# Hybrid-decoder step on one core: dilated attention's loads joined (both heads, both halves), v kept a second time by residue, and two SBUF pools exchanged

## The chip, the cores and the metric

The kernel runs on one core of a Trainium2 chip, as one launch. The metric is the device time of that launch in microseconds. Before the change it is 3003.89 us, the median of three runs (3002.21 to 3005.41).

## The reference, cut to what matters

One decoder layer is computed for 2048 prompt tokens and for 32 new tokens of eight running requests, all in float32. `h + concat(HGRN2, DilatedAttention) @ w_o`, then a gated convolutional FFN, then a per-layer embedding gate. The change lies in the prompt's dilated attention:

```
DILATIONS = ((128, 1), (512, 4), (2048, 16))
for window, dil in DILATIONS:
    # positions of one residue class mod dil form a sub-sequence;
    # a query reads the last window/dil + 1 entries of its own
    s = where(valid, q*scale @ k.T, -1e30); m = s.max(-1); p = exp(s - m)
    parts.append((m, p.sum(-1), p @ v))
w = exp(ms - ms.max(0))
out = (w[..., None] * accs).sum(0) / (w * ls).sum(0)[..., None]
```

There are 8 heads of 64 numbers. The kernel works on four pairs of heads p, and on four chunks c of 512 tokens.

## The kernel before, in words

The program has three stretches, told apart in the profile by their lines.

**Input projection (up to about 826 us).** `in_phase` runs twice, on two blocks of tokens, and multiplies the normalised input with seven groups of weights. `token_group` handles q, k, v and i by tiles of 128 tokens: 24 matmuls (L345 to L347), a scaled copy into `ev` (L358), for q and k a rotation and four transposes into `oT`, and then stores into DRAM scratch. L374 stores a tile of q or k into `qT_d` or `kT_d`, laid out [128 rows of a head pair, 4 pairs, 2048 tokens], so that a tile makes runs of 512 bytes. L383 and L384 store a tile of v to its output and to `v_d` [2048, 512].

**Attention (about 826 to 1195 us).** `attn_phase` goes through the four pairs. For each pair and chunk:

- `stage` (L684 to L693) brings q and k in, two tiles [128 partitions, 2 heads, 512]. Both halves of the partitions get the same data, so that one matmul can multiply two precision parts of q. It takes four DMAs, one for each half of each tile, 256 KB each. Pool `a_d` holds four such tiles. `stack` (L695) splits them into `qS`, `kH` and `kL` on ACT and POOL.
- `values_chunk` (L726) brings v in twice: for di = 0 as [128, 4 residues, 128] in one DMA (L731), for di = 1 with the rows of a residue side by side, in four DMAs of 32 partitions (L734).
- 16 `Block`s of 128 queries each pass through `scores` (L803, matmuls L811 and L812, the masked minimum L816 on DVE, which reads `mask`, and the exponential L817 on ACT), `turned` (transposes L824) and `weighted` (L836).
- `merge` (L740 to L775) joins the two softmaxes of a chunk. Their statistics go to DRAM and come back turned (L889, L742); small steps give 16 rows of coefficients, which go to `coef_d` (L763) and come back spread over the partitions in `cf` [128, 2, 512]: two DMAs, one for each head, each reading 4 KB for 64 partitions (L767). POOL multiplies (L772), DVE or POOL adds (L774), and the result is stored to `mix_d` (L775).

Beside it a second generator, `others`, does the last HGRN2 unit and the attention of the 32 new tokens, which reads 32 tiles of 1 MB each (`skt`, L940 and L976).

**Trunk (from about 1201 us).** `trunk` does w_o, FFN and embedding gate. Its first weights are read into pool `tr`, seven buffers `raw` of 2 KB per partition (L1004), and split into `w` (L181, L182); its first activations come from `mix_d` (L1098) and are split by L1080 and L1081.

**What sets the order.** In the attention stretch PE's order is written out by the program. The order on the other engines, and on SyncE (SP), which issues nearly all DMAs, comes from a planner that runs over the whole program. An SP instruction that waits holds up all that stand behind it.

**SBUF.** Pools are put on a stack, each above the one opened before, and a new tile waits for the tiles whose place it takes. Per partition, `early` has 8448 bytes: small constants, the rotary table, at offset 2304 the `mask` of 3072 bytes, then the new tokens' q, k and v. `rows` above it has 8448 bytes: `ssq` and `rb` of the input projection, used again for the very first stage. When attention ends both are closed and the trunk's pools take their place: `ffn_c` 1952 bytes with padding, then `raw` buffer 0 at offset 1952, buffer 1 at 4000, and so on. Buffers 0 and 1 thus lie on the mask.

Of the kernel before, what the change touches and what calls it, by code (L numbers as in the profile page):

```python
# [11 lines left out]
F32 = mybir.dt.float32  # L12
# [10 lines left out]
SEQ = 2048  # L23
# [24 lines left out]
def hymba_step_kernel(ctx: ExitStack, tc: tile.TileContext, I: dict, O: dict):  # L48
    nc = tc.nc
    V, A, G, PE, SP = nc.vector, nc.scalar, nc.gpsimd, nc.tensor, nc.sync  # L50

    const = ctx.enter_context(tc.tile_pool(name="const", bufs=1))
    dram = ctx.enter_context(tc.tile_pool(name="scratch", bufs=1, space=DRAM))

    early_st = ExitStack()
    early = early_st.enter_context(tc.tile_pool(name="early", bufs=1, reuse_waits="tile"))

# [21 lines left out]
    v_s = early.tile([NS, 512], F32, name="v_s")  # L79
    va_s = const.tile([NS, 512], F32, name="va_s")  # L80

    qT_d = dram.tile([128, 4, SEQ], F32, name="qT_d")
    kT_d = dram.tile([128, 4, SEQ], F32, name="kT_d")
    v_d = dram.tile([SEQ, 512], F32, name="v_d")
    va_d = dram.tile([SEQ, 512], F32, name="va_d")
    ha_d = [dram.tile([128, 4, NTOK], F32, name=f"ha{i}_d") for i in range(3)]
# [7 lines left out]
    def f32(ap):  # L94
        return ap.bitcast(F32)
# [89 lines left out]
    recent = []  # L185
# [35 lines left out]
    def in_phase(bi, tiles, shared, wp, ev, sm, pmm, pms, plv, po):  # L221
# [102 lines left out]
        def token_group(g, kind, w):  # L324
            late = None

            for j in (0, 1, 8, 2, 3, 4, 5, 6, 7) if bi else range(8):
                tok = t0 + 128 * j
                n = min(128, T - 128 * j)
                js = slice(128 * j, 128 * j + n)  # L330
                ps = acc_tile()
                smp = n < 128
                if smp:

                    terms = [(xs[:, k], f32(w[k][i])) for k in range(NK) for i in range(2)]
                    side = 128 // n
                    for i, (a, b) in enumerate(terms):
                        c = n * (i % side)
                        PE.matmul(ps[c:c + n], lhsT=a, rhs=b, start=i < side, stop=i >= len(terms) - side,
                                  tile_position=(0, c))  # L340
                else:
                    side = 1
                    for k in range(NK):
                        wh, wl = w[k]
                        PE.matmul(ps, lhsT=xh[k][:, js], rhs=wh, start=k == 0, stop=False)  # L345
                        PE.matmul(ps, lhsT=xh[k][:, js], rhs=wl, start=False, stop=False)  # L346
                        PE.matmul(ps, lhsT=xl[k][:, js], rhs=wh, start=False, stop=k == NK - 1)  # L347
                if late:
                    late()
                    late = None  # L350
                sc = rq if kind == "q" else rc
                if smp and kind == "v":
                    o = v_s
                elif smp and kind == "i":
                    o = va_s
                else:
                    o = ev.tile([128, 512], F32, name="ev", bufs=4)
                A.activation(o[:n], ps[:n], AF.Copy, scale=sc[:n, j:j + 1])  # L358
                for i in range(1, side):
                    V.scalar_tensor_tensor(o[:n], ps[n * i:n * i + n], sc[:n, j:j + 1], o[:n], op0=ALU.mult, op1=ALU.add)  # L360
                if kind in "qk":
                    rotate(o, 16 if smp else tok // 128, n)

                    def late(o=o, n=n, smp=smp, tok=tok):
                        pt = pms.tile([128, 512], F32, name="ms")
                        ptv = pt.rearrange("p (a t) -> p a t", t=128)
                        for p in range(4):
                            PE.transpose(ptv[:, p, :n], o[:n, 128 * p:128 * p + 128], ident[:n, :n])
                        if smp:
                            V.tensor_copy(qT_s if kind == "q" else kT_s, ptv[:, :, :n])  # L370
                        else:
                            oT = ev.tile([128, 4, 128], F32, name="oT", bufs=2)
                            V.tensor_copy(oT, ptv)
                            recent[:] = [SP.dma_start((qT_d if kind == "q" else kT_d)[:, :, tok:tok + 128], oT)]  # L374
                if smp:
                    if kind in "kv":
                        for b in range(8):
                            SP.dma_start(O["s" + kind][b, SEQ - 4:SEQ], o[4 * b:4 * b + 4])
                else:
                    if kind == "k":  # L380
                        SP.dma_start(O["pk"][tok:tok + 128], o)
                    if kind == "v":
                        SP.dma_start(O["pv"][tok:tok + 128], o)  # L383
                        recent[:] = [SP.dma_start(v_d[tok:tok + 128], o)]  # L384
                    if kind == "i":
                        SP.dma_start(va_d[tok:tok + 128], o)
                yield
            if late:
                late()
# [292 lines left out]
    def attn_phase(spare, rest):  # L682

        def stage(p, c, tiles=()):  # L684

            out = []
            for i, src in enumerate((qT_d, kT_d)):
                t = tiles[i] if tiles else dp.tile([128, 2, 512], F32, name="stage", bufs=4)
                for half in range(2):
                    SP.dma_start(t[64 * half:64 * half + 64],  # L690
                                 src[:, p, 512 * c:512 * c + 512].rearrange("(h d) t -> d h t", h=2))
                out.append(t)
            return out  # L693

# [20 lines left out]
        q, k = first  # L715
# [10 lines left out]
        def values_chunk(p, di, c):  # L726

            raw = wk.tile([128, 4, 128], F32, name="v", bufs=6)
            cols = v_d[512 * c:512 * c + 512, 128 * p:128 * p + 128]
            if di == 0:  # L730
                SP.dma_start(raw, cols.rearrange("(i r) c -> i r c", r=4))  # L731
            else:
                for r in range(4):
                    SP.dma_start(raw[32 * r:32 * r + 32], cols.rearrange("(n i r) c -> r i n c", i=32, r=4)[r])  # L734
            vals[p, di, c] = raw

        stats_d = [dram.tile([SEQ, 4], F32, name=f"stat{p}_d") for p in range(4)]
# [2 lines left out]
        def merge(p, c, parts, both):  # L740

            SP.dma_start(both[:, 0].rearrange("p n h c -> p n (h c)"),  # L742
                         stats_d[p][512 * c:512 * c + 512].rearrange("(n i) c -> i n c", i=128))
            stats = both.rearrange("p i n h c -> p c h i n")
            spread = lambda x: x.rearrange("p h (o n) -> p h o n", o=1).to_broadcast([128, 2, 2, 4])
            yield
            mn = sm.tile([128, 2, 4], F32, name="mn")
            w = sm.tile([128, 2, 2, 4], F32, name="w")
            wl = sm.tile([128, 2, 2, 4], F32, name="wl")
            V.tensor_reduce(mn, both.rearrange("p i n h c -> p c h n i")[:, 1], axis=mybir.AxisListType.X, op=ALU.min)  # L750
            G.tensor_sub(w, spread(mn), stats[:, 1])
            A.activation(w, w, AF.Exp)
            yield
            G.tensor_mul(wl, w, stats[:, 0])
            G.tensor_add(mn, wl[:, :, 0], wl[:, :, 1])
            V.reciprocal(mn, mn)
            G.tensor_mul(w, w, spread(mn))
            yield
            ptr = pT.tile([128, 4, 128], F32, name="PT")[:16, 0]
            PE.transpose(ptr, w.rearrange("p h d n -> p (h d n)"), ident)  # L760
            wt = sm.tile([16, 128], F32, name="wt")
            A.copy(wt, ptr)
            SP.dma_start(coef_d[p][c], wt)  # L763

            cf = wk.tile([128, 2, 512], F32, name="cf", bufs=2)
            for h in range(2):
                SP.dma_start(cf[64 * h:64 * h + 64].rearrange("p d i -> p (d i)"),  # L767
                             coef_d[p][c][8 * h:8 * h + 8].rearrange("(o r) i -> o (r i)", o=1)
                             .to_broadcast([64, 1024]))
            yield  # L770
            for i in range(2):
                G.tensor_mul(parts[i], parts[i], cf[:, i])  # L772
            yield
            (G if p == 3 else V).tensor_add(parts[1], parts[1], parts[0])  # L774
            SP.dma_start(mix_d[:, 4 + p, 512 * c:512 * c + 512], parts[1])  # L775
# [73 lines left out]
        n = len(units)  # L849
# [717 lines left out]
    def pools(st, **kw):  # L1567
        def pool(name, bufs, **k):
            return st.enter_context(tc.tile_pool(name=name, bufs=bufs, reuse_waits="tile", **kw, **k))
        return pool  # L1570

    rows_st, in_st, hgrn_st, attn_st = [ExitStack() for _ in range(4)]
    rows = pools(rows_st)("rows", 1)
    pool = pools(in_st)
    args = (in_tiles(pool("xp", 1), rows), [], pool("wp", 9), pool("ev", 2), pool("sm", 1),
            pool("pmm", 2, space=PSUM), pool("pms", 2, space=PSUM))
# [80 lines left out]
        first(side, 1000)  # L1657
    step(main, 1000)
    attn_st.close()
    rows_st.close()  # L1660

    early_st.close()
    with ExitStack() as st:
        pool = pools(st)
        cp = pool("ffn_c", 1)
# [153 lines left out]
```

## Time and profile before

| what | value |
|---|---|
| median of three runs | 3003.89 us |
| the profiled execution's own time | 3008.49 us |
| its span, first to last instruction | 3006.7 us |
| mean TensorE clock granted | 0.981 |
| PE busy | 2908.9 us |
| DVE / ACT / POOL busy | 2166.4 / 1319.2 / 676.9 us |
| DMA moved | 664.14 MB |
| SP issues of `stage` loads after 820 us | 60, of 256 KB |
| SP issues of `cf` loads | 32, of 256 KB |
| SP issues of `v` loads | 16 of 256 KB, 64 of 64 KB |

How to read it: the device time is a little longer than the span, because of what lies around the first and the last instruction. PE's busy share says how near the kernel is to being bound by matmuls, but it is a mean over the three stretches. "DMA share" in the tables below is the mean over the core's 16 DMA engines, so a transfer that keeps two of them busy all the time shows as 0.125. Packets are the single pieces that a DMA engine moves; q1 is the queue into which SP issues.

### The profile page before, as it was taken

The numbers are of one execution on the slowest core, as the hardware profiler recorded it, in microseconds if no ns is written. First come the engines' busy times: TensorE is split into PE (matmuls) and PEld (weight loads), VectorE is DVE, ScalarE is ACT, GpSimd is POOL, SyncE is SP. The second block draws the span as 40 slices with busy tenths as digits, with TensorE's granted clock in tenths as the row PEclk, the third lists the DMA queues.
The fourth block names the chain that finished last, engine by engine and source line by source line (L and its number), as shares of the span: only waits on it lengthen the run. The fifth ranks groups of instructions, "written<-read, shape, count | busy, mean of one in ns | idle before, by whom it ended". The sixth has DMA issues, their size and how long they took to land.

```text
span 3006.7 us, 52441 instructions
## 1 busy us (share of the span) xinstructions
PE 2908.9 (97%) x18895; PEld 2711.0 (90%) x18895; DVE 2166.4 (72%) x4717; ACT 1319.2 (44%) x2856; POOL 676.9 (23%) x792
## 2 busy tenths in 40 slices
PE   8999999999989998999999999999999999999998
PEld 8987789887777677999999999999999999999997
DVE  6656768657386567569988889766769777777777
ACT  5333433222176666335444444544444544444453
POOL 1443222212143463102344431000001000000000
PEclk9999999999989999999999999999999999999998
DMA  5898634323349996766666568677779777778773
GB/s 183 297 359 299 202 103 120 99 86 121 122 107 286 276 249 177 260 224 220 224 206 196 191 198 302 227 252 250 246 230 321 240 242 246 257 249 295 269 274 131
DMA packets 343061, 664.14 MB, mean 221 GB/s; under 512 B 62929, under 2 KB 130641, under 8 KB 341009
## 3 DMA queue, kind: packets, MB, share of 16 engines
q1 hardware_dynamic: 305952, 472.68, 48.4%
q0 software_dynamic: 33264, 121.13, 12.6%
q10 hardware_dynamic: 3584, 66.98, 6.1%
q8 instruction: 149, 2.44, 0.3%
q14 instruction: 112, 0.91, 0.1%
HBM read 513.72 MB, written 213.92 MB: 242 GB/s over the span
## 4 chain that ended last, share of the span: by engine, by line
PE 78%; DVE 9%; DMA 7%; issue 2%; ACT 2%; POOL 1%; SPq 1%; DVEq 0%; POOLq 0%; ACTq 0%
PE mm L143 19%; PE mm L144 19%; PE mm L145 19%; PE mm L345 2%; PE mm L346 2%; PE mm L347 2%; PE acc L836 2%; PE PT L824 2%; PE S L811 1%; DVE h L1305 1%; PE S L812 1%; PE lv L482 1%; DMA wraw<-in_w_in_dram 1%; DMA cf<-coef_d 1%; DMA draw<-in_w_down_dram 1%
## 5 line engine op out<-in xcount | busy, mean ns | idle before, releaser
L144 PE MATMUL mm<-w 128*128 128x348 f32 (+3 forms) x3636 | 1167.6, 322 | 1.9 <-DVE w L1081 1.1
L143 PE MATMUL mm<-w 128*128 128x348 f32 (+3 forms) x3508 | 1111.4, 323 | 21.2 <-ACT s L1247 6.7
L145 PE MATMUL mm<-w 128*128 128x348 f32 (+3 forms) x3508 | 1118.9, 322 | 0.7 <-DVE w L182 0.7
L144 PEld LDWEIGHTS mm<-w 128*128 128x128 f32 x3636 | 685.4, 189 | 4.9 <-DVE w L1081 3.0
L143 PEld LDWEIGHTS mm<-w 128*128 128x128 f32 x3508 | 658.2, 189 | 29.7 <-ACT s L1247 9.3
L145 PEld LDWEIGHTS mm<-w 128*128 128x128 f32 x3508 | 660.2, 189 | 1.8 <-DVE w L182 1.0
L182 DVE TENSOR_TENSOR w<-raw,w 128x512 fp32r<-128x512 f32 x586 | 420.8, 723 | 180.8 <-ACT w L181 175.7
L181 ACT CAST w<-raw 128x512 fp32r<-128x512 f32 x586 | 360.9, 621 | 414.5 <-PE mm L145 286.4
L1289 POOL DMA_DIRECT2D w<-wd_d x231 | 123.8, 536 | 900.1 <-PE mm L145 794.1
L1305 DVE TENSOR_TENSOR h<-h,mm 128x348 f32<-128x348 f32 (+1 forms) x504 | 248.7, 510 | 44.7 <-PE mm L145 43.1
L817 ACT ACTIVATE P<-P,st 128x256 f32<-128x256 f32 (+3 forms) x256 | 134.1, 526 | 67.2 <-DVE st L816 62.6
L1247 ACT COPY s<-mm 128x348 f32<-128x348 f32 (+1 forms) x198 | 87.9, 444 | 158.1 <-PE mm L145 158.0
L816 DVE CUSTOM_DVE_ANT_0 P<-S,mask 128x256 f32<-128x256 f32 (+3 forms) x256 | 104.4, 448 | 62.2 <-PE S L812 39.5
L345 PE MATMUL mm<-wh,xh 128*128 128x512 f32 x352 | 141.0, 404 | 0.0
L346 PE MATMUL mm<-wl,xh 128*128 128x512 f32 x352 | 140.5, 400 | 0.0
L347 PE MATMUL mm<-wh,xl 128*128 128x512 f32 x352 | 140.3, 399 | 0.0
L143 PE MATMUL mm<-xh,wh 128*128 128x384 f32 (+2 forms) x384 | 124.5, 328 | 7.0 <-ACT xh L243 5.0
L145 PE MATMUL mm<-xh,wl 128*128 128x384 f32 (+2 forms) x384 | 124.1, 328 | 4.7 <-DVE wl L268 4.6
L144 PE MATMUL mm<-xl,wh 128*128 128x384 f32 (+2 forms) x384 | 124.8, 327 | 1.3 <-DVE xl L244 1.2
L182 DVE TENSOR_TENSOR dw<-draw,dw 128x512 fp32r<-128x512 f32 x77 | 73.0, 954 | 52.7 <-ACT dw L181 52.6
L149 POOL TENSOR_SCALAR wh<-wraw 128x512 fp32r<-128x512 f32 x96 | 77.4, 820 | 131.6 <-PE mm L144 42.4
L268 DVE TENSOR_TENSOR wl<-wraw,wh 128x512 fp32r<-128x512 f32 x104 | 84.5, 833 | 28.6 <-POOL wh L149 23.3
(346 smaller groups left out, 5090.9 us busy)
## 6 DMA issues: line engine op xcount, KB each, us to landing
w<-wd_d POOLq DMA_DIRECT2D x231, 512.0 KB, 5.5
wd_d<-dw SPq DMA_DIRECT2D x77, 512.0 KB
out_sk_dram<-in_cache_k_dram ACTq DMA_DIRECT2D x56, 584.0 KB
out_sv_dram<-in_cache_v_dram ACTq DMA_DIRECT2D x56, 584.0 KB
raw<-in_w_gate_dram SPq DMA_DIRECT2D x110, 256.0 KB
raw<-in_w_up_dram SPq DMA_DIRECT2D x110, 256.0 KB
wraw<-in_w_in_dram SPq DMA_DIRECT2D x104, 256.0 KB
raw<-w_gate_d SPq DMA_DIRECT2D x88, 256.0 KB
```

The source lines that it names most:

```text
L143: PE.matmul(ps, lhsT=wh, rhs=xh, start=first, stop=False, skip_group_check=read)
L144: PE.matmul(ps, lhsT=wh, rhs=xl, start=False, stop=False, skip_group_check=read)
L145: PE.matmul(ps, lhsT=wl, rhs=xh, start=False, stop=last, skip_group_check=read)
L181: A.copy(w[:, 0], raw)
L182: V.tensor_sub(w[:, 1], raw, f32(w[:, 0]))
L345: PE.matmul(ps, lhsT=xh[k][:, js], rhs=wh, start=k == 0, stop=False)
L346: PE.matmul(ps, lhsT=xh[k][:, js], rhs=wl, start=False, stop=False)
L347: PE.matmul(ps, lhsT=xl[k][:, js], rhs=wh, start=False, stop=k == NK - 1)
L816: V.tensor_tensor_reduce(pe, s[:, w * i:w * i + w], bl.mask, 1.0, 3e38, ALU.add, ALU.min, mn)
L817: A.activation(pe, pe, AF.Exp, bias=mn, scale=-1.0, accum_out=st[:, bl.r, hh, 0:1])
L1289: G.dma_start(t, wd_d[p][n - 1])
L1305: V.tensor_add(o, o, acc[m][:, :H])
```

## The change

`qT_d` and `kT_d` are laid out by chunks, so that the two heads' 512 tokens of one row and chunk stand together as 4 KB, and a tile is stored in two DMAs, one for each head. A stage tile is then filled by one DMA of 512 KB instead of two of 256 KB: its source is the 64 rows of 4 KB, repeated by an outermost dimension of size 2 with step 0. v is stored once more, in `v_r`, with the rows of each 128 ordered by residue, so that the di = 1 load is one DMA too. `cf` is filled by one DMA whose source has the head outermost (2), then 64 repeats of one 4 KB row. Pool `rows` is opened before `early`, so it lies below it.

```
-    qT_d = dram.tile([128, 4, SEQ], F32, name="qT_d")
-    kT_d = dram.tile([128, 4, SEQ], F32, name="kT_d")
+    qT_d = dram.tile([64, 4, 4, 2, 512], F32, name="qT_d")
+    kT_d = dram.tile([64, 4, 4, 2, 512], F32, name="kT_d")
+    v_r = dram.tile([SEQ, 512], F32, name="v_r")
...
-    recent[:] = [SP.dma_start((qT_d if kind == "q" else kT_d)[:, :, tok:tok + 128], oT)]
+    for h in range(2):
+        dst = (qT_d if kind == "q" else kT_d)[:, :, tok // 512, h, tok % 512:tok % 512 + 128]
+        recent[:] = [SP.dma_start(dst, oT[64 * h:64 * h + 64])]
...
-    recent[:] = [SP.dma_start(v_d[tok:tok + 128], o)]
+    SP.dma_start(v_d[tok:tok + 128], o)
+    recent[:] = [SP.dma_start(v_r[tok:tok + 128].rearrange("(r i) c -> i r c", r=4), o)]
...
-    for half in range(2):
-        SP.dma_start(t[64 * half:64 * half + 64],
-                     src[:, p, 512 * c:512 * c + 512].rearrange("(h d) t -> d h t", h=2))
+    half = src[:, p, c].rearrange("(o d) h t -> o d (h t)", o=1)
+    SP.dma_start(t.rearrange("d h t -> d (h t)"), half.to_broadcast([2, 64, 1024]))
...
-    for r in range(4):
-        SP.dma_start(raw[32 * r:32 * r + 32], cols.rearrange("(n i r) c -> r i n c", i=32, r=4)[r])
+    cols = (v_d, v_r)[di][512 * c:512 * c + 512, 128 * p:128 * p + 128]
+    SP.dma_start(raw, cols.rearrange(("(i r) c -> i r c", "(r i) c -> i r c")[di], r=4))
...
-    for h in range(2):
-        SP.dma_start(cf[64 * h:64 * h + 64].rearrange("p d i -> p (d i)"),
-                     coef_d[p][c][8 * h:8 * h + 8].rearrange("(o r) i -> o (r i)", o=1)
-                     .to_broadcast([64, 1024]))
+    SP.dma_start(cf.rearrange("p d i -> p (d i)"),
+                 coef_d[p][c].rearrange("(h o r) i -> h o (r i)", h=2, o=1).to_broadcast([2, 64, 1024]))
...
+    rows_st = ExitStack()
+    rows = rows_st.enter_context(tc.tile_pool(name="rows", bufs=1, reuse_waits="tile"))
     early_st = ExitStack()
...
     attn_st.close()
+    early_st.close()
     rows_st.close()
-
-    early_st.close()
```

More of the change, by code (lines that the diff above doesn't have):

```diff
@@ L728, in values_chunk @@
             raw = wk.tile([128, 4, 128], F32, name="v", bufs=6)
[L729 to L732, printed above, removed]
-                for r in range(4):
-                    SP.dma_start(raw[32 * r:32 * r + 32], cols.rearrange("(n i r) c -> r i n c", i=32, r=4)[r])
+            cols = (v_d, v_r)[di][512 * c:512 * c + 512, 128 * p:128 * p + 128]
+            SP.dma_start(raw, cols.rearrange(("(i r) c -> i r c", "(r i) c -> i r c")[di], r=4))
             vals[p, di, c] = raw
@@ L1570, in pools @@
         return pool
-    rows_st, in_st, hgrn_st, attn_st = [ExitStack() for _ in range(4)]
-    rows = pools(rows_st)("rows", 1)
+    in_st, hgrn_st, attn_st = [ExitStack() for _ in range(3)]
     pool = pools(in_st)
```

## The prediction

> **What bounds the kernel now.** I read the page first, for the engines and the time slices.
>
> ```profile
> span 3006.7 us, 52441 instructions
> PE 2908.9 (97%) x18895; PEld 2711.0 (90%) x18895; DVE 2166.4 (72%) x4717; ACT 1319.2 (44%) x2856; POOL 676.9 (23%) x792
> ...
> PE   8999999999989998999999999999999999999998
> ...
> DMA  5898634323349996766666568677779777778773
> ```
>
> PE is busy for 97% of the span. A slice is 75 us; the DMA engines' three nines, the 13th to the 15th slice, and their peak in the 2nd to 4th are the only places where transfers could be the limit. So I cut the attention stretch out and asked for the busy time in windows. The columns are PE, PEld, DVE, ACT, POOL, granted clock, DMA share, GB/s.
>
> ```profile
> 822.00:850.00 28.00, 19.63 (x92) 16.08 (x91) 19.40 (x57) 15.70 (x37) 20.10 (x18) 0.72 0.88 232
> 850.00:900.00 50.00, 46.82 (x438) 40.80 (x436) 40.04 (x130) 37.23 (x110) 14.54 (x17) 0.94 0.20 45
> 900.00:1100.00 200.00, 186.63 (x1616) 136.38 (x1617) 117.95 (x422) 125.31 (x363) 94.44 (x112) 0.93 0.98 276
> 1100.00:1202.00 102.00, 88.55 (x820) 74.66 (x820) 70.70 (x260) 64.76 (x197) 41.87 (x61) 0.94 0.68 186
> 1202.00:1210.00 8.00, 6.87 (x24) 6.20 (x24) 8.00 (x7) 4.22 (x7) 5.22 (x4) 0.52 0.56 184
> ```
>
> From 900 to 1100 us the 16 DMA engines are 98% busy while PE is 93% busy: there both are near their limit, and DMA has no room to spare. Then the transfers of 822 to 1202 us: the queue's total (packets, MB, share of 16 engines' time) and the loads that the change touches.
>
> ```profile
> q1 hardware_dynamic: 74718, 82.48, 78.1%
> ...
> stage<-qT_d SPq DMA_DIRECT2D x30, 256.0 KB
> ```
>
> ```profile
> cf<-coef_d SPq DMA_DIRECT2D x32, 256.0 KB
> stage<-kT_d SPq DMA_DIRECT2D x30, 256.0 KB
> v<-v_d SPq DMA_DIRECT2D x16, 256.0 KB
> v<-v_d SPq DMA_DIRECT2D x64, 64.0 KB
> ```
>
> 78.1% of 380 us is 297 us of work for each engine, and the 60 stage and 32 cf loads are 92 x 0.262 = 24.1 of the 82.5 MB. Last, what PE itself waited for in that stretch, the first and the fourth row of its list:
>
> ```profile
> PE mm L143 <- ACT w L1080: 6.5, 1, 6.5
> ...
> PE s L942 <- DMA skt<-in_kT_d_dram: 4.3, 2, 4.0
> ```
>
> So at present PE sets the time, transfers come second, and the largest single stop is the step into the trunk.
>
> **The stage and cf loads: on how many engines?** This decides the case. Two windows in the input projection show how one DMA is dealt out: eight stores of four rows each, and then two stores of 128 rows each.
>
> ```profile
> DMA packets 64, 0.07 MB, mean 15 GB/s; under 512 B 32, under 2 KB 32, under 8 KB 64
> ...
> out_sv_dram<-v_s SPq DMA_DIRECT2D x8, 8.0 KB
> ```
>
> ```profile
> DMA packets 288, 0.52 MB, mean 131 GB/s; under 512 B 32, under 2 KB 32, under 8 KB 288
> ...
> q1 hardware_dynamic: 288, 0.52, 34.0%
> ...
> out_pv_dram<-ev SPq DMA_DIRECT2D x1, 256.0 KB
> v_d<-ev SPq DMA_DIRECT2D x1, 256.0 KB
> ```
>
> The two large stores are 256 packets of data and 32 small ones, so 16 small packets for one DMA, as many as there are engines: I read them as each engine's note that its share is done. The eight small stores are 32 packets of data and 32 small ones: four for each DMA. So a DMA whose outermost dimension is 4 runs on four engines. The new stage and cf loads have 128 partitions outermost at the destination, but 2 outermost at the source. The trace has no load with unlike sides, so it does not show which side counts; an engine needs a share cut out on both sides, and I take the smaller: two engines. The Trainium skill says this outright ("DMA: Bandwidth & Descriptors", section "Rules for kernel authors"): an outermost dimension of fewer than 16, with a zero-step repeat as its own example, keeps the whole DMA on at most so many engines. The four-row stores agree with that, four engines for four rows; no run here shows it for a repeated source. By it the sum is the one below; without it, it is that of the first rival.
>
> Next, what one engine moves. The densest six microseconds, 914 to 920 us, and a stretch of 12 us from 854 us that holds almost nothing but four stage loads:
>
> ```profile
> DMA packets 1169, 2.30 MB, mean 384 GB/s; under 512 B 51, under 2 KB 51, under 8 KB 1168
> ...
> q1 hardware_dynamic: 1168, 2.29, 104.3%
> ```
>
> ```profile
> q1 hardware_dynamic: 720, 1.06, 36.9%
> ```
>
> The first gives 384 / (16 x 1.043) = 23.0 GB/s for one engine, the second 1.06 MB / (0.369 x 12 us x 16) = 15.0, and the whole stretch 82.48 MB / (0.781 x 380 us x 16) = 17.4. The slow ones are 16 engines at once, many of them reading the same rows; two engines with 14 others mostly idle are nearer to the first row. I take 23.0, and keep 17.4 for the range.
>
> At 23.0 a load of 0.524 MB on two engines takes 11.4 us, a q and k pair 22.8. The two engines get 24.1 / 2 = 12.06 MB, which is 524 us, and a sixteenth of the other 58.9 MB (without the pair of cf loads issued after the window), 160 us: 684 us of work, against the 380 us of the stretch now. None of it can start earlier: the stage buffers come free only when the input projection ends. Nor can the others help, since every 16-engine DMA also waits for its share on these two. So **+304 us**; at 17.4 it is 693 + 211 = 904 us, so +524. PE's work there, 341.6 us, fits in 684 even at half clock, so it stays hidden.
>
> On top come the places where the two engines run dry, because SP waits for a small store before it may issue the load that reads it back:
>
> ```profile
> SPq L742 <- DMA stat_d<-st: 4.3, 3, 2.4
> ...
> SPq L767 <- DMA coef_d<-wt: 5.0, 5, 1.6
> ```
>
> That is 1.2 us each; there are 32 such pairs, so 0 to 37 us. Once the queue is always full they all show, so I take +37. Taken off: two cf loads that no longer hold up the trunk's first block, 2 x 11.4 = **-23**.
>
> **Issues saved and added.** The SP rows for the loads and stores, with the time that one issue holds SP (least, median, most, in ns):
>
> ```profile
> L690 SPq DMA_DIRECT2D stage<-qT_d x30: 573/605/3178, 822.2 to 1101.7; - x30
> L767 SPq DMA_DIRECT2D cf<-coef_d x32: 450/562/1452, 952.6 to 1202.7; - x32
> L734 SPq DMA_DIRECT2D v<-v_d x64: 302/428/2017, 835.6 to 1175.7; - x64
> L374 SPq DMA_DIRECT2D qT_d<-oT x16: 513/525/1176, 231.8 to 734.4; - x16
> L384 SPq DMA_DIRECT2D v_d<-ev x16: 319/472/1391, 182.2 to 827.2; - x16
> ```
>
> Attention loses 30 stage, 16 cf and 48 v issues: 18 + 9 + 21 = 48 us of SP. That is worth nothing here, because SP then waits for the engines. The di = 1 load keeps 128 partitions outermost, and so 16 engines and the same bytes. The input projection gains 32 half stores of q and k and 16 stores of v_r: 17 + 8 = 25 us of SP over 600 us, and 16 x 0.68 us of the engines (half of the 34.0% of 4 us that two such stores took) = 11 us, under PE's nines. Cover gone, it would be those 11 us. A v tile's `ev` buffer is held for one store longer, 0.7 us of a tile time many times that. The two very first stage loads, one for each tile, go out in the input projection:
>
> ```profile
> 379.23 1.29 SPq L690 DMA_DIRECT2D ssq<-qT_d  x2
> ...
> 623.05 1.24 SPq L690 DMA_DIRECT2D rb<-kT_d  x2
> ```
>
> Each tile will now hold two engines for 11.4 us, and weight loads queue behind the second: 0 to 11 us, I take +4.
>
> **The exchange of the pools.** The step into the trunk, from the timelines of DVE, SP, PE and ACT:
>
> ```profile
> 1189.20 0.42 DVE L816 CUSTOM_DVE_ANT_0 P<-S,mask 128x256 f32<-128x256 f32 x1
> ...
> 1189.65 0.81 SPq L1004 DMA_DIRECT2D raw<-in_w_o_dram  x2
> ...
> 1194.67 2.20 SPq L1004 DMA_DIRECT2D raw<-in_w_o_dram  x3
> ...
> 1194.74 0.28 PE L760 MATMUL PT<-c_ident,w 128*16 128x128 f32 x1
> ...
> 1200.21 0.62 ACT L181 CAST w<-raw 128x512 fp32r<-128x512 f32 x1 [2.50 <-DMA raw<-in_w_o_dram]
> ```
>
> The first two `raw` loads go at 1189.65, the moment the mask has been read for the last time; the sixth goes at 1194.67, its cast runs at 1200.21, ACT's split of the activations comes behind it, and PE stands for 6.5 us. With `rows` below, buffers 0 to 3 lie on `rows` and on the constants under the mask, all long free, and only 4 and 5 (offsets 10144 to 14240, the mask at 10752) wait. The loads can go 5 us earlier, so up to 6 of the 6.5 us come back, and 2 to 4 us of the clock of 0.52 that follows. Against it, they may stand behind a cf load of 11.4 us. Bounds -10 to +11; I take **-6**.
>
> Sum: 304 + 37 - 23 + 4 - 6 = +316 on the profiled execution's own 3008.5 (span 3006.7), so 3324.5. That execution lies 4.6 us above the median of the runs, so 3320 for the median.
>
> **The rivals.** *The loads spread over 16 engines after all* (the destination's 128 counts, or the repeat is folded away). For it: the destination does have 128 rows. Against it: the four-row stores. Then 6 to 10 us come back at the step into the trunk and 48 us of SP give perhaps 2 us of the 4.3 us that PE waits for `skt`: 3008.5 - 10, so 2994 for the median, and faster. It decides at the first stage load at 822 us: landed within 3 us it is this, after 11 us it is the forecast. The same page and section of the Trainium skill has a rule that speaks for it, one transfer to 128 partitions rather than two to the halves; the rows give the 48 us of issue time and nothing more for it.
>
> *Only the stage loads are confined* (two distinct rows count otherwise than a repeat). 15.7 MB / 2 at 23.0 is 342 us and a sixteenth of the other 66.8 MB 181 us: 523 us, +143, about 3147; at 17.4 +312. Nothing in the trace parts the two.
>
> *The change does nothing*: the loads spread, and the raws wait for something else than the mask. 3004, within 3 us. Against it: the raws' issue at the mask's last read, to 0.1 us.
>
> **How the numbers follow.** Forecast 0.74, stage only 0.07, spread 0.15, nothing 0.04. About 0.2%, 6 us, is what a measurement of this kernel can tell from no change. Faster by over that 0.15, within it 0.04, slower 0.81. The range leaves out the two cases that are not slower, 0.19, and reaches from the stage-only sum less 7 us, 3140, to the 17.4 GB/s sum with the round trips, the first loads and the worst step: 3008.5 + 524 + 37 + 11 less what overlaps, 3580; it is that of the likeliest case too, whose fast end, 3265, lies inside.
>
> **What would show it.** Right: attention from 822 us to the first trunk matmul takes about 690 us; the DMA share there falls to about 0.45 while PE, ACT and POOL wait for `stage` and `cf`; a stage load leaves two small packets, not 16; the 1 MB `skt` loads land late; input projection and trunk keep their times. Wrong: a share near 0.9 with the stretch at 370 to 380 us (the spread), or 20 to 30% shares with PE waiting on SP's small stores (then round trips, not the two engines, are the price).

## The result, and the profile after

The changed kernel takes 3315.94 us (median of six runs, 3312.57 to 3324.58), the kernel before 3001.33 us beside it (six runs): a ratio of 1.1047 [1.103, 1.1064]. The profiled execution's span grew from 3006.7 to 3316.8 us, by 310.1.

The page of the changed kernel, its span, the engines' busy times, and the slices of PE, of PE's granted clock and of the DMA engines:

```profile
span 3316.8 us, 52351 instructions
...
PE 2948.4 (89%) x18895; PEld 2731.2 (82%) x18895; DVE 2152.9 (65%) x4717; ACT 1318.4 (40%) x2856; POOL 665.5 (20%) x792
...
PE   8999999999464546577999999999999999999998
...
PEclk9999999999686777688999999999999999999999
DMA  5899343244234435346666666787777977777784
```

Two things go down together from the 11th to the 19th slice (a slice is 83 us now): PE, from nines to fours to sevens, and DMA, from the three nines of before to between two and six. A stretch in which transfers kept all 16 engines busy would show high DMA digits; here both are low. So something waits, and the 16 engines' mean does not show what for. Outside these slices little has changed.

The same stretch in windows, from PE's first score matmul of attention to the trunk's first matmul: after, then the trunk's first 46 us, and before. The columns are PE, PEld, DVE, ACT, POOL, granted clock, DMA share, GB/s.

```profile
821.22:1494.06 672.84, 377.51 (x2944) 285.30 (x2944) 238.26 (x865) 239.27 (x703) 164.30 (x201) 0.74 0.40 122
1494.00:1540.00 46.00, 28.90 (x162) 28.20 (x163) 9.66 (x14) 7.77 (x13) 8.81 (x8) 0.80 0.48 169
```

```profile
827.89:1201.56 373.67, 337.12 (x2944) 264.50 (x2944) 246.54 (x864) 240.81 (x703) 168.62 (x203) 0.91 0.79 219
```

The same 2944 matmuls take 672.84 instead of 373.67 us. The books close: attention starts 6.7 us earlier (821.22 against 827.89), it lasts 299.2 longer, and one stop of 17.05 us in the trunk's first block, which before does not have, adds the rest: 309.6 of 310.1. PE's own work grew by 40 us, while the granted clock fell from 0.91 to 0.74; with 295 us of idle time beside it, that is covered.

Where the two engines can be seen: the DMA view of the changed kernel over 11 us in which SP issues one stage load and two small stores. The first row is 40 slices of 0.275 us.

```profile
DMA  1111111111111111311111111111111111141111
...
DMA packets 271, 0.61 MB, mean 55 GB/s; under 512 B 128, under 2 KB 128, under 8 KB 270
...
q1 hardware_dynamic: 270, 0.59, 13.6%
...
stage<-kT_d SPq DMA_DIRECT2D x1, 512.0 KB
stat_d<-st SPq DMA_DIRECT2D x2, 8.0 KB
```

The share stays at one tenth for slice after slice: 13.6% of 16 engines is 2.2 engines, two that are always busy and now and then a small store. 0.59 MB in 11 us is 53.6 GB/s, 26.8 for each, so a load of 0.524 MB takes 9.8 us here. Counted from the packet records of the stretch, with other traffic in it, a 4 KB packet takes 173.3 ns in the mean, and a load's 64 packets per engine 11.1 us. The small end-of-share packets agree: with 1662 DMAs on that queue, 16 four-row stores with four of them, and 48 loads (32 stage, 16 cf) with two, there would be 26592 - 192 - 672 = 25728, and 25728 are there. The Trainium skill says how the number comes about ("DMA: Bandwidth & Descriptors", section "Why a DMA increments its semaphore by 16 and not by 1"): the largest number up to 16 that divides the slowest dimension of both sides. For 2 and 128 that is 2, and the trace agrees with it.

What the chain of waits consists of in the stretch, after and then before, by line (the profile cuts the row off). Below the first row stand the five longest pieces of the chain after, each with its start and length in us:

```profile
by line: DMA cf<-coef_d 18.2%; DMA stage<-kT_d 13.0%; DMA skt<-in_kT_d_dram 9.0%; issue 5.6%; DMA stage<-qT_d 5.4%; DMA coef_d<-wt 4.4%; DMA skt<-in_kT_w_dram 3.5%; SPq L735 3.3%; PE acc L835 3.1%; PE PT L823 3.1%; PE S L810 2.8%; POOL o L7
...
1046.36 26.35 DMA cf<-coef_d
1095.14 25.39 DMA cf<-coef_d
1160.68 25.87 DMA stage<-kT_d
1228.31 28.91 DMA cf<-coef_d
1332.89 29.00 DMA stage<-kT_d
```

```profile
by line: PE acc L836 13.3%; PE PT L824 12.8%; PE S L811 10.9%; PE S L812 7.6%; DMA cf<-coef_d 5.6%; DMA skt<-in_kT_d_dram 5.2%; PE s L942 3.7%; PE s L979 2.9%; issue 2.9%; ACT P L817 2.8%; DMA st<-stat_d 2.6%; PE s L659 2.3%; DMA coef_d<-wt
```

Before, matmuls head the chain. After, cf and stage loads are 36.6% of it, and PE's three lines 9%. The longest pieces last 25 to 29 us, more than twice what a load takes by itself (9.8 us). That fits a load that also stands behind other transfers on its two engines; the chain does not part the two. PE itself, though, names neither of the loads. The head of its list of waits from 815 to 1520 us, and below it two rows of the list for all engines:

```profile
PE PT L823 <- ACT P L816: 65.8, 6, 13.7
PE s L941 <- DMA skt<-in_kT_d_dram: 56.0, 7, 10.2
PE S L810 <- DVE st L815: 48.0, 7, 16.1
...
POOL o L771 <- DMA cf<-coef_d: 288.5, 14, 70.7
...
ACT kH L709 <- DMA stage<-kT_d: 123.8, 9, 17.7
```

PE waits for `P`, for the minimum `st`, and for `skt`, a load that the change did not touch. The cause stands one step further back, with ACT and POOL, which make PE's operands.

Last the step into the trunk, on PE and on SP:

```profile
1494.06 0.95 PE L146 MATMUL mm<-w 128*128 128x348 f32 x2 [3.71 <-ACT w L1079]
...
1538.69 0.66 PE L148 MATMUL mm<-w 128*128 128x348 f32 x1 [17.05 <-DVE w L185]
```

```profile
1490.49 4.67 SPq L1003 DMA_DIRECT2D raw<-in_w_o_dram  x5
...
1508.05 0.51 SPq L767 DMA_DIRECT2D cf<-coef_d  x1
1508.65 16.38 SPq L774 DMA_DIRECT2D mix_d<-o  x2
...
1534.36 0.33 SPq L1003 DMA_DIRECT2D raw<-in_w_o_dram  x1
```

The first stop is shorter than before's 6.54 us. But SP's store of the last merge waits 16.4 us, since the last cf load is late, and the next `raw` loads stand behind that store until 1534.36; `w` and PE follow.

### The profile page after: what moved, and what is told of

Its sections match the earlier page's. It is cut to its first block, busy times and chain, and to the rows that moved or that the text cites. A ratio compares the mean times of both kernels' runs of the same rounds, so it can differ in the third digit from the quotient of the medians.

```text
span 3316.8 us, 52351 instructions
## 1 busy us (share of the span) xinstructions
PE 2948.4 (89%) x18895; PEld 2731.2 (82%) x18895; DVE 2152.9 (65%) x4717; ACT 1318.4 (40%) x2856; POOL 665.5 (20%) x792
## 4 chain that ended last, share of the span: by engine, by line
PE 69%; DMA 16%; DVE 7%; SPq 3%; issue 2%; ACT 2%; POOL 1%; DVEq 0%; POOLq 0%; ACTq 0%
PE mm L146 17%; PE mm L148 17%; PE mm L147 17%; DMA cf<-coef_d 4%; DMA stage<-kT_d 3%; PE mm L348 2%; PE mm L349 2%; PE mm L350 2%; DMA skt<-in_kT_d_dram 2%; DMA coef_d<-wt 1%; DMA stage<-qT_d 1%; DVE h L1304 1%; DMA xr<-in_xT_dram 1%; PE lv L488 1%; DMA skt<-in_kT_w_dram 1%
## 5 line engine op out<-in xcount | busy, mean ns | idle before, releaser
L823 PE MATMUL PT<-c_ident,P 128*128 128x128 f32 x568 | 95.4, 314 | 106.8 <-ACT P L816 65.8
L823 PEld LDWEIGHTS PT<-c_ident,P 128*128 128x128 f32 x568 | 77.2, 162 | 116.7 <-ACT P L816 69.5
L810 PE MATMUL S<-kH,qS 128*128 128x256 f32 (+3 forms) x256 | 105.5, 425 | 50.2 <-DVE st L815 48.0
L810 PEld LDWEIGHTS S<-kH,qS 128*128 128x128 f32 x256 | 68.5, 268 | 97.7 <-DVE st L815 54.4
```

What stands on the lines that cost most here:

```text
L810: PE.matmul(s[:, w * i:w * i + w], lhsT=bl.q(hh), rhs=bl.k(kH, hh), start=True, stop=False)
L823: PE.transpose(pt[:, i], self.pe[:, 128 * i:128 * i + 128], ident)
```

## The experiments

The kernel before was run beside each of them on the same chip, and each ratio is to it. A load is called confined where its outermost dimension of 2 keeps it on two engines.

**1. Only cf confined** (`e1_cf_confined_only`): the changed kernel, with a stage tile loaded in two DMAs of 64 rows.

```
-                SP.dma_start(t.rearrange("d h t -> d (h t)"), half.to_broadcast([2, 64, 1024]))
+                for half in range(2):
+                    SP.dma_start(t[64 * half:64 * half + 64].rearrange("d h t -> d (h t)"), src[:, p, c]...)
```

> Theory (two engines): only the cf loads still have an outermost dimension of 2; the stage loads are two DMAs of 64 rows again, with the 4 KB rows of the new layout. Two engines then have 16 x 64 packets of 0.173 us = 177 us plus a sixteenth of the other 74 MB, 200 to 266 us: 377 to 443 us for a stretch of 375 us before. So 3005 to 3070 us, the excess where DVE and POOL wait for cf. Small packets of the queue rise by 16 x 14 fewer lost ones. Rival (repeated rows are slow in themselves, whatever the split): cf repeats as before, so no change against the kernel before, 3001. Rival (the price is the new order on SP and its waits for small stores): most of the 315 us stay, above 3200.

**2. Only stage confined** (`e2_stage_confined_only`): the changed kernel, with cf in two DMAs, one for each head.

```
-            SP.dma_start(cf..., coef_d[p][c].rearrange("(h o r) i -> h o (r i)", h=2, o=1).to_broadcast([2, 64, 1024]))
+            for h in range(2):
+                SP.dma_start(cf[64 * h:64 * h + 64]..., coef_d[p][c][8 * h:8 * h + 8]....to_broadcast([64, 1024]))
```

> Theory (two engines): only the stage loads keep an outermost dimension of 2. 30 x 64 x 0.173 = 332 us plus a sixteenth of the other 67 MB, 181 to 240 us: 513 to 572 us, so 138 to 197 us over the kernel before, 3140 to 3200 us; together with the cf-only run the two excesses should not quite add up to 315, as each alone fills the two engines less. Rival (repeated rows are slow in themselves): about the same as this, so it is not told apart here. Rival (SP's order): near 3316 or near 3001, with no relation to the bytes.

**3. Neither confined** (`e3_none_confined`): both edits; new layouts, v and pools stay.

> Everything of the change but the two outermost dimensions of 2: layouts by chunk, v_r, pools exchanged; stage and cf loads as two DMAs of 64 rows each. Theory (two engines): the whole 315 us are gone; 2985 to 3000 us, a little under the kernel before, from the step into the trunk and 48 fewer v loads. Rival (SP's order, or the layouts themselves): part of the 315 us stays.

Measured: 3115.86 us, ratio 1.0374 [1.0354, 1.0394]; 3192.47 us, 1.0632 [1.0609, 1.0655]; 2996.88 us, 0.9979 [0.9966, 0.9993]. The attention stretch of each, in this order:

```profile
824.04:1293.07 469.03, 353.24 (x2943) 276.78 (x2943) 242.37 (x865) 239.90 (x703) 165.73 (x201) 0.87 0.63 173
```

```profile
821.38:1384.89 563.51, 360.15 (x2944) 275.58 (x2944) 242.85 (x865) 239.43 (x703) 164.97 (x201) 0.78 0.48 145
```

```profile
825.45:1188.37 362.92, 327.43 (x2943) 256.71 (x2944) 245.70 (x865) 239.57 (x703) 166.50 (x201) 0.96 0.81 224
```

With both pairs of loads split again the whole loss is gone, and 7.8 us (2 to 10 by the interval) are won. So the two kinds of load are the loss, all of it. Against the 362.92 us of the third kernel, cf alone adds 106.1, stage alone 200.6, both 309.9: they add up (306.7). Stage alone came as expected. cf alone did not: it is 46 us above the top of what was expected. Counted from the packet records, a packet is under way in 416 of its 469 us, which is within the 377 to 443 us that were expected for the whole stretch; in the other 53 us none is. The third kernel also has 53 us without a packet, in 363, so the added 106 us are all time with packets under way. What the expectation left out is the time in which nothing moves.

**4. Two outermost, but no repeat** (`e5b_two_outermost_no_repeat`): q and k are stored twice, and the stage load reads the two copies, with an outermost dimension of 2 and a step that isn't 0; cf split.

```
-    qT_d = dram.tile([64, 4, 4, 2, 512], F32, name="qT_d")
+    qT_d = dram.tile([2, 4, 4, 64, 2, 512], F32, name="qT_d")
...
-                SP.dma_start(t.rearrange("d h t -> d (h t)"), half.to_broadcast([2, 64, 1024]))
+                SP.dma_start(t.rearrange("d h t -> d (h t)"), src[:, p, c].rearrange("a b h t -> a b (h t)"))
```

> q and k are written twice into scratch (4 MB more of stores), so a stage load is one DMA of 512 KB whose source names 128 different rows, but with an outermost dimension of 2 again (step not zero); cf in two loads. Theory (the outermost count of 2 sets two engines): as the stage-only run within 20 us, 3130 to 3200. Rival (it is the repeat, the same rows read twice, that makes the load slow): 2990 to 3010.

**5. Four outermost** (`e5d_four_outermost`): the same two copies, cut into four pieces of 32 rows.

```
-    qT_d = dram.tile([2, 4, 4, 64, 2, 512], F32, name="qT_d")
+    qT_d = dram.tile([4, 4, 4, 32, 2, 512], F32, name="qT_d")
```

> q and k written twice into scratch, one stage load of 512 KB with an outermost dimension of 4, no repeat; cf in two loads. Theory (outermost count = engines): four engines, 32 packets each, 5.5 us a load. If the price is the work on the confined engines, 60 x 0.262 / 4 = 3.9 MB, 171 us plus 181 to 240: 352 to 411 us for a stretch of 375, so 3000 to 3035. If it is the time that each load takes on the chain, it should fall with that time: a pair 11 us instead of 22, so a third to a half of the 190 to 213 us, 3060 to 3100. Rival (one load of 512 KB is slow whatever its outermost count): 3190 to 3220.

Measured: 3217.77 us, 1.0718 [1.0698, 1.0738], and 3118.12 us, 1.0382 [1.0366, 1.0398]. The stretches:

```profile
850.98:1412.48 561.50, 359.04 (x2943) 274.59 (x2943) 241.96 (x865) 239.48 (x703) 164.94 (x201) 0.78 0.48 145
```

```profile
866.29:1310.48 444.19, 350.11 (x2943) 268.98 (x2943) 241.51 (x865) 239.19 (x703) 165.18 (x201) 0.86 0.62 183
```

561.50 us without a repeat, 563.51 with one: what counts is the size of the outermost dimension, not that its step is 0. With four engines the stretch is 81 us over the third kernel's instead of 200. The end-of-share packets show the four: with 1870 DMAs on the queue, the 16 four-row stores and 32 loads with four packets each, there would be 29920 - 192 - 384 = 29344, and 29344 are in the packet records.

Both times lie above what was expected, 3217.77 us above 3200 and 3118.12 above 3100. Both kernels also start attention later, at 850.98 and 866.29 us instead of 821.38 in experiment 2 and 825.45 in 3. That fits their input projection, which now makes twice and four times the stores of q and k, though nothing else tested it; the delay of 30 and 41 us is more than what they lie above, and it is why only the stretches are compared. Less its 41 us, experiment 5 is in the range that was named for the time of each load, 3060 to 3100, and not in that for the engines' work, 3000 to 3035. But of its 444.19 us a packet is under way in 397, which is inside the 352 to 411 us of that work; the rest is time in which nothing moves.

The Trainium skill ("DMA: Bandwidth & Descriptors", section "Rules for kernel authors") gives a repeat as its example of a small outermost dimension; these two runs agree, and show it for a real second copy too.

**6. The exchange of the pools alone** (`e4_exchange_alone`): the kernel before, with `rows` opened before `early` and closed after it, nothing else.

```
+    rows_st = ExitStack()
+    rows = rows_st.enter_context(tc.tile_pool(name="rows", bufs=1, reuse_waits="tile"))
     early_st = ExitStack()
...
+    early_st.close()
     rows_st.close()
-
-    early_st.close()
```

> The kernel before with nothing but the pools exchanged (rows below early). If the gain of the run without confined loads (-8 us) is the step into the trunk: 2994 to 2999 beside 3001 to 3004, and PE's stop there falls from 6.5 to about 3.4 us. Rival (the gain comes from the layouts and the 48 fewer v loads): no difference.

**7. The layouts alone** (`e10_layouts_alone`): the third kernel with that edit taken back.

> As the run without confined loads, but with the pools as before: layouts by chunk, v_r and one load for each v tile alone. If the exchange makes the gain: within 3 us of the kernel before. Rival: 5 to 8 us under it. The input projection has 48 more stores; it should keep its time.

Measured: 3000.5 us, 0.9989 [0.9979, 0.9998], and 2997.93 us, 0.9981 [0.9968, 0.9994]. The trunk's first matmul in each:

```profile
1198.47 0.92 PE L145 MATMUL mm<-w 128*128 128x348 f32 x2 [2.53 <-ACT w L1082]
```

```profile
1195.42 0.95 PE L144 MATMUL mm<-w 128*128 128x348 f32 x2 [7.63 <-ACT w L1080]
```

The exchange does what it says: the stop goes from 6.54 to 2.53 us, and stays (7.63) where the pools are left alone. It is worth 3 us (1 to 6 by the interval), a little less than expected. The layouts with v's fewer loads are worth 5.6 (2 to 10). Both gains are near the bound of what can be measured.

**8. cf used later** (`e9_cf_confined_later_use`): the first kernel, with the last two steps of each merge eight steps later.

```
-                    merge_at([x + d for d in (0, 2, 3, 7, 10, 11)], p, c, (outs[c], o), bl.both)
+                    merge_at([x + d for d in (0, 2, 3, 7, 18, 19)], p, c, (outs[c], o), bl.both)
```

> The cf-only run (cf on two engines, stage split) with the last two steps of a merge, the multiplication and the addition, eight turns later in the program, so that cf has some 18 us more to land. If the cf load costs because DVE waits in order behind it (the chain: addition, multiplication, cf): most of the 111 us go, 3005 to 3040. If it costs because two engines have too much to move: unchanged, 3100 to 3120. Both leave the stop at the trunk's start, where SP stands behind the last store of a merge.

Measured: 3116.57 us, 1.0378 [1.036, 1.0396], as without the edit. It decides nothing: DVE still waits 101.0 us in 12 times for the multiply behind cf, where the first kernel has 105.0 in 12, and POOL's multiplies run within 2 us of where they ran there, so the planner had put the instructions where they had been.

**9. The adds off DVE** (`e11_cf_confined_adds_on_pool`): in the first kernel DVE waits for cf's multiply, with PE's minimum queued behind it. Here POOL adds for all four pairs.

```
-            (G if p == 3 else V).tensor_add(parts[1], parts[1], parts[0])
+            G.tensor_add(parts[1], parts[1], parts[0])
```

> The cf-only run with the sixteen additions of the merges all on POOL (before, twelve of them are on DVE, where they wait 105 us behind cf and hold PE's operands). If the cf load costs by holding DVE (the chain): 3010 to 3050, as PE's waits for DVE vanish. If the confined engines are full (two engines carry 169 us of cf and 274 of the rest in 469 us, 94%): the waits move elsewhere, to stage, v and skt, and the time stays within 20 us of 3116.

PE's waits for DVE's minimum in the first kernel, and the head of PE's list in this one:

```profile
PE S L811 <- DVE st L816: 50.5, 9, 9.9
```

```profile
PE s L979 <- DMA skt<-in_v_d_dram: 25.8, 4, 9.6
PE PT L824 <- ACT P L817: 25.2, 7, 7.3
PE s L618 <- DVE hsF L430: 21.5, 1, 21.5
...
PE S L811 <- DVE st L816: 4.0, 3, 1.9
```

Measured: 3120.31 us, 1.0387 [1.0365, 1.041]. The wait of 50.5 us was taken away, to 4.0, and not one microsecond came back: others took its place. So the additions on DVE are not what cf costs, and the time stayed within 20 us of 3116, as was expected if the two engines are full. One link is left as it was: POOL still waits for cf in its multiplies, 200.2 us in 14 times from 815 to 1300 us against 207.1 in the first kernel, with its other work behind them. What that holds up was not tested.

**10 and 11. Less work for the two engines** (`e12_changed_fewer_skt`, and `e13_before_fewer_skt` as its control): the changed kernel and the kernel before, each with 24 of the 32 `skt` loads of 1 MB left out.

```
-                    kt = kp.tile([128, 4, 512], F32, name="skt")
-                    SP.dma_start(kt, I[src][4 * g:4 * g + 4, :, p]...)
+                    if p == 0:
+                        kt = kp.tile([128, 4, 512], F32, name="skt")
+                        SP.dma_start(kt, I[src][4 * g:4 * g + 4, :, p]...)
```

> The changed kernel with 24 of the 32 loads of 1 MB for the new tokens' attention left out: one tile of keys or values is read for each four and used for all four, so the new tokens' attention is computed from the wrong rows; the arithmetic and the PE order are the same. Takes 25.2 MB, 1.57 MB for each engine, 68 to 90 us, off the two full engines. If their work sets the time (capacity): 3225 to 3260 from 3316. If each stage and cf load costs by its own 11 us on the chain: no more than the same edit does to the kernel before.

> The control: the kernel before with the same 24 loads left out and the same wrong rows for the new tokens. There PE sets the time and DMA has a share of 0.79 in the stretch: 2980 to 3000, so 5 to 20 us.

Measured: 3297.49 us, 1.0972 [1.0953, 1.099], and 2986.55 us, 0.9938 [0.992, 0.9955]: 18 us less than the changed kernel (22 by the two ratios), and 18 less than the kernel before. The stretches:

```profile
826.59:1477.37 650.78, 369.58 (x2944) 284.50 (x2944) 237.09 (x865) 239.32 (x703) 163.25 (x201) 0.74 0.27 87
```

```profile
827.42:1183.49 356.07, 327.45 (x2943) 259.10 (x2943) 242.56 (x864) 240.26 (x703) 168.24 (x203) 0.95 0.60 159
```

24 loads leave 24 x 65.5 KB less for each engine, 68 us at 23 GB/s. The time with any packet under way fell by about that, from 647 to 577 us of the stretch (counted from the packet records). The stretch fell by 22 us, and 48 us turned into time in which no packet moves at all, which rose from 26 to 74 us. The kernel before, where nothing is confined, gains nearly as much (17.6). So the amount of the two engines' work is not by itself what sets the end.

**12. Stage loads issued by ACT** (`e14_stage_on_act_queue`): is it that everything stands behind the stage loads in SP's one queue?

```
-                SP.dma_start(t.rearrange("d h t -> d (h t)"), half.to_broadcast([2, 64, 1024]))
+                A.dma_start(t.rearrange("d h t -> d (h t)"), half.to_broadcast([2, 64, 1024]))
```

> The changed kernel with the stage loads issued from ACT's queue instead of SP's; same loads, same two engines, nothing left out. If what makes the two confined kinds so dear is that everything else from SP stands behind them in one queue (an issue of a v load holds SP 4.1 us at the median instead of 0.4, a coefficient store 3.3 instead of 0.36), the other loads get past them: 3150 to 3260. If the loads' own 11 us on the chain are the price, or the two engines' work: 3296 to 3330. Slower than that, if ACT is held at each issue as SP was (30 issues of 2 to 9 us on an engine that is busy 239 of 673 us).

One issue of the same 256 KB v load (least, median, most, in ns) in the kernel before and in the changed kernel, and then two rows of this one, for v and for stage. The 0.4 us in the expectation is that of the 64 KB loads of v.

```profile
L731 SPq DMA_DIRECT2D v<-v_d x16: 541/577/1197, 830.4 to 1149.2; - x16
```

```profile
L735 SPq DMA_DIRECT2D v<-v_d x16: 527/4074/9458, 848.2 to 1434.8; - x16
```

```profile
L735 SPq DMA_DIRECT2D v<-v_d x16: 517/703/14727, 846.4 to 1449.7; - x16
```

```profile
L696 ACTq DMA_DIRECT2D stage<-kT_d x15: 489/490/19259, 820.7 to 1342.0; - x15
```

Measured: 3330.56 us, 1.1095 [1.1075, 1.1114]. SP is freed, from 4.07 to 0.70 us for a median v issue, and the time does not fall. That speaks against SP's order as the price, but does not rule it out: ACT is now held by the issues itself, for up to 19.3 us at once and 107 us over the 30 of them, and a gain could be hidden under that. 3330.56 us lies on the edge between the two cases that were expected without a gain: the loads' own price (up to 3330) and ACT held at its issues (above).

## Why the prediction was right, point by point

**Two engines: right, and for the reason given.** With 2 and with 4 at the source and 128 at the destination the smaller of the two outermost dimensions counts. The windows, the count of small packets and experiments 4 and 5 show it; other pairs of sizes were not run. The rival that the loads spread (2994) is what experiment 3 gives with four halves instead of two joined loads: 2996.88. The rival of stage alone was a real price (190 us over the stretch of the kernel before; 143 was reckoned), but cf is confined too. As for the Trainium skill's rule of one transfer to 128 partitions in place of two to the halves ("DMA: Bandwidth & Descriptors", section "Rules for kernel authors"): it did not hold here, since the joined load had 2 outermost; stage joined against stage split is 3192.47 against 2996.88 us.

**+304, 684 us of work in the stretch: the size was right, the step not wholly.** 672.84 us were measured, with a packet under way in 647 of them, and the load's 11.4 us was 9.8 to 11.1. An estimate from the packet records, which name no engine: the 45 confined loads that fall into the stretch are 499 us of packets for each of two engines, and a sixteenth of all other packets 202, so 701 in 673 us (packets overlap a little). In the changed kernel the two engines are thus as good as full. The time with a packet under way also fits the work that was reckoned in the smaller cases: 416 us in experiment 1 (377 to 443), 537 in 2 (513 to 572), 397 in 5 (352 to 411).

What is not borne out is the step that their work alone is the length: between 26 and 53 us in which nothing moves come on top in these four kernels, and 74 in experiment 10. If work alone counted, experiment 10 would have won at least 56 us by its expectation, and won 18, as much as its control; the same estimate gives 597 us of packets there, in 651. What fits as well is that a load's own time stands in the chain of waits: cf alone adds 106.1 us for 16 x 11.1 = 178 us of loads, stage alone 200.6 for 30 x 11.1 = 333, both 309.9 for 511. That is 0.60, 0.60 and 0.61 of it. With four engines it is 81 us for 30 loads of 32 packets, 0.49 of their time with the same 173.3 ns a packet and 0.41 with the 206 ns of that kernel's own mean, so the share is not a constant. In the full case chain and capacity lie close together, which is why the sum came out; to that extent it is luck. That a load's time is in the chain is a fit through four kernels and the chain of waits, and the cause of the length stays open between the two: experiment 9 came out as full engines would have it, experiment 10 did not. More stage buffers, which would have tested the chain directly, were not tried. Which link of the chain keeps 0.6 and hides 0.4 stays open too: experiment 9 rules out the additions on DVE, experiment 12 speaks against SP's queue, experiment 8 did not test what it was made for, and POOL's order was not tried.

**+37 for round trips: the waits are there, but not on top.** SP's waits for the two small stores (two in each of 16 merges) went from 4.3 + 5.0 to the rows below, so +27.7. They lie inside the 299.2 by which the stretch grew, where +304 and +37 make 341:

```profile
SPq L743 <- DMA stat_d<-st: 19.3, 4, 11.2
...
SPq L767 <- DMA coef_d<-wt: 17.7, 5, 8.2
```

**-23 for the last two cf loads: wrong sign.** They were taken off the sum, as loads that do not hold up the trunk's first block. They hold SP at the last merge's store, and the trunk's weights behind it: a stop of 17.05 us. It comes with cf's confinement: the stop is 15.7 us in experiment 1 and 15.3 in 10, but 1.7 in 2 and 3.

**+4 for the first stage loads: not seen.** The input projection ended 6.7 us earlier. Apart from experiments 4 and 5 with their added stores, the kernels with the new layouts begin attention between 821 and 827 us, in no order that an edit explains, so this is left open.

**-6 for the exchange: right mechanism, half the size.** The first stop fell by 2.8 us in the changed kernel (6.54 to 3.71) and by 4.0 alone, for 3 us of time.

**Nothing for 48 us of saved issues: right here**, where SP waits for the engines anyway. Where nothing is confined, layouts and v's 48 fewer issues bring 5.6 us. **PE's work stays hidden: right**, 377.51 of 672.84 us.

The errors partly cancel: the terms of the sum gave +316, and the profiled spans differ by 310. +304 and +37 were 42 us too much for the stretch, and the -23 came out as +17, 40 us too little; that the sum lies within 6 us is luck. Of the range, the fast end of 3265 us has no working in the prediction, and 3580 is the plain sum of its terms, with nothing taken off for overlap.

## What to carry to other kernels

Before two DMAs are joined, write down the outermost dimension of both sides of the new one: if it is 2, the load runs on two of 16 engines, whether that dimension is a repeat or a second copy, and one issue of 0.6 us saved is paid with a load of 10 us instead of one spread over 16. Two low digits at once, PE's and DMA's, with a share that sits at one tenth, are how it looks in a profile. The version to keep is that of experiment 3, with new layouts, v by residue and exchanged pools, and two 64-row loads for each stage and cf tile: 2996.88 us, 0.9979 [0.9966, 0.9993].

## What the runs showed of the hardware

- An issue itself takes longer when two engines are behind: a 256 KB v load goes to all 16 engines, and its issue took 4.07 us in the median after, against 0.58 us before and 0.57 in experiment 3. From ACT a stage issue took up to 19.3 us, against 0.49 at the least.
- A 4 KB packet took 159 ns in the median in the changed kernel's stretch, and 258 in experiment 3's, where 16 engines mostly work at once. So in these kernels an engine moves such a packet faster when few others work beside it. Both numbers are counted from the packet records.
- The granted clock was lower where PE idled much more: 0.74 with 295 us of idle time in the stretch (both loads confined), 0.78 with 203 (stage alone), 0.87 with 116 (cf alone). Idle time alone does not set it: it is 0.91 before and 0.96 in experiment 3, with 37 and 35 us.
